# Attention of a hybrid decoder: fixed tiles for split transposes and probabilities, weights loaded one unit ahead, residual rows on VectorE

## The chip, the cores and the metric

The kernel runs on one core of a Trainium2 chip. The core has five engines that run their own instruction queues in order: TensorE (PE in the profile) for matrix products, VectorE (DVE), ScalarE (ACT), GpSimd (POOL) and SyncE (SP, which here only starts transfers). Data is worked on in the on-chip memory; matrix products land in eight accumulation banks. The metric is the device time of one execution in microseconds (us), lower is better.

## The reference

A trunk of two layers runs over 1024 tokens of width 1024 in float32. The even layer mixes with a pooling and a state-space part, the odd layer with two kinds of causal attention; behind each mixer stand a layer norm and a SwiGLU block (FFN) with another norm. The change touches the odd layer above all:

```python
def block_causal_attention(q, k, v, log_decay_cum):   # 8 heads of 64, twice
    ...
        sc = jnp.einsum('bhqd,bhkd->bhqk', qi, k).astype(F32) * scale
        if fi is not None:
            sc = sc + fi[..., :, None] - log_decay_cum[:, :, None, :]
        sc = jnp.where(kpos[None, :] <= qpos[:, None], sc, -jnp.inf)
        p = jax.nn.softmax(sc, axis=-1).astype(v.dtype)
        return jnp.einsum('bhqk,bhkd->bhqd', p, v)
...
    x = layer_norm(DEEPNORM_ALPHA * x + h, ln_mix_g[l], ln_mix_b[l])
    x = layer_norm(DEEPNORM_ALPHA * x + swiglu(x, ffn_w_gate[l], ffn_w_up[l], ffn_w_down[l]),
                   ln_ffn_g[l], ln_ffn_b[l])
```

The first kind of attention has a forget gate (the bias `log_decay_cum`), the second has its queries and keys unpacked from a low-rank latent.

## The kernel before

**Products.** Every float32 operand is split into a high and a low part by `split` or `operand`: ScalarE writes the high part (line 196), VectorE or GpSimd subtracts it from the source (line 204). Each product is then three matmuls: high by high, high by low, low by high (lines 237 to 239 in the projections, 499 to 501 and 635 to 637 in the FFN).

**The pool of slots.** One pool, `big`, of 50 slots of 128 x 1024 float32 holds nearly everything: raw weights `wr`, their parts `wh` and `wl`, probabilities `prob`, split transposes `pt`, squares `sq` for the norm of the latents, residual rows `resr`. A call of `slot` takes a new slot; the first instruction that writes it waits until all users of the slot's former tile are done. Each engine takes its queue in order, so such a wait holds up everything behind it on that engine.

**Attention.** `weave` interleaves two generators. `chain` goes through four pairs of heads of the first kind and four of the second; a step is a head and a block of 256 queries. `softmax` makes the scores (TensorE, line 1600), their minimum or maximum on VectorE, the exponential on ScalarE and the division on VectorE (line 1631). `pv` then transposes the probabilities on TensorE (line 1652), splits the transposes into a `pt` tile (or into the one fixed tile `diag` where the causal edge lies), and multiplies by the values (line 1670). `filler` supplies projection units for the heads to come; `preload` loads raw weights `ahead + dma_ahead` units ahead and splits them `ahead` units ahead. In time: the first kind of attention fills some 1230 to 1590 us of the trace, the second some 1590 to 1840.

**Residual rows.** The even layer's FFN left its normed rows without gain and offset in the DRAM tensor `store`. `late` loads each of the eight row blocks, multiplies by the gain, adds the offset (lines 442 and 443) and stores it again (line 444); `chain` calls it once in every second step from the second pair on. The odd layer's end reads the rows back as `acc` (line 1510).

**FFN.** `ffn` multiplies 2 x 2 blocks with seven products in place of eight. The product `step` takes its accumulation bank from `bank()`, which goes round a list; `second` is the down projection and begins with banks `p0` to `p3`.

Of the kernel before, what the change touches and what calls it, by code (L numbers as in the profile page):

```python
# [12 lines left out]
F32 = mybir.dt.float32  # L13
F32R = mybir.dt.float32r
BF16 = mybir.dt.bfloat16
AF = mybir.ActivationFunctionType
ALU = mybir.AluOpType
# [64 lines left out]
class Trunk:  # L82
# [67 lines left out]
    def turn(self, tags):  # L150
        self.turns[tags] = n = self.turns.get(tags, -1) + 1
        return self.ps(tags[n % len(tags)], 1)
# [238 lines left out]
    def finish(self, accs, gb, evac, ln=None, store=None, nxt=None, rows=None):  # L391
# [3 lines left out]
        nc = self.nc  # L395
# [41 lines left out]
        def late():  # L437
            v = self.ln_vecs(*gb)
            yield
            for t in range(NT):  # L440
                r = self.load_raw(store[t * P:(t + 1) * P, :], name="res")
                nc.gpsimd.tensor_tensor(out=r, in0=r, in1=v[0], op=ALU.mult)
                nc.gpsimd.tensor_tensor(out=r, in0=r, in1=v[1], op=ALU.add)
                nc.gpsimd.dma_start(out=store[t * P:(t + 1) * P, :], in_=r)
                yield
# [3 lines left out]
    def ffn(self, l, ln, store, rows, parts, nxt=None):  # L449
# [53 lines left out]
        hid = {}  # L503
        turn = itertools.cycle(("p0", "p1", "p2", "p3", "pa", "pa"))

# [717 lines left out]
    def odd(self, accs, store, spill, nxt, rows):  # L1223
# [350 lines left out]
        def filler():  # L1574
            self.grain = self.odd_grain
            misc_weight()
            self.preload(units, self.pre_n, ws)
            for g, u in zip(lead, units):
                yield from g
                done.add(u[0])  # L1580
            yield from spread(self.units_y(units, done, ws, 2), self.spread)
# [26 lines left out]
        def softmax(S, nF):  # L1608
            prob = []
            n = [x.shape[1] for x in S]  # L1610
            if sum(n) <= 1024:
                t = self.slot(name="prob")
                prs = [t[:, :n[0]], t[:, n[0]:n[0] + n[1]]]
            else:
                prs = [self.slot(name="prob")[:, :x] for x in n]
            l = self.small((P, 2), "l", bufs=6)
# [19 lines left out]
        for t in diag:  # L1636
            for c in (0, 512):
                nc.vector.tensor_copy(out=t[:, c:c + P], in_=self.zerob)

        def pv(prob, vv, u, ot, e):  # L1640
            nj = 2 * u + 2
            hl = {}

            def tr(jj):
                ps = self.pb()
                last = jj == u
                for y in range(2):
                    j = 2 * jj + y
                    for x in range(2):
                        c = (1 - y if last else y) * 256 + x * P  # L1650
                        if j <= 2 * u + x:
                            nc.tensor.transpose(out=ps[:, c:c + P], in_=prob[x][:, j * P:(j + 1) * P],  # L1652
                                                identity=self.ident)
                t = diag[self.turn_of("diag", self.n_diag)] if last else self.slot(dt=F32R, name="pt")
                b = P if last else 0
# [71 lines left out]
        def chain():  # L1727
# [4 lines left out]
            n = 0  # L1732
            for pr in pairs():
# [5 lines left out]
                for i, (e, u) in enumerate(self.steps[kind]):  # L1739
# [5 lines left out]
                    if pend and self.tr_first[kind]:  # L1745
                        next(pend[0])
                    if n and i % 2:
                        next(late, None)
# [143 lines left out]
```

## Time and profile before

| what | value |
|---|---|
| three executions, us | 2543.9, 2545.56, 2548.15 (median 2545.56) |
| the profiled execution, us | 2546.77 |
| its span in the trace, us | 2544.7 |
| TensorE busy, us (share of the span) | 2449.8 (96%) |
| VectorE | 1824.6 (72%) |
| ScalarE | 1044.6 (41%) |
| GpSimd | 758.2 (30%) |
| mean granted clock of TensorE | 0.986 of 2.4 GHz |

The span is the traced part of the profiled execution. The shares are means over the whole program; the stages differ. A granted clock of 1.00 stands for 2.4 GHz, and one near 0.50 for the lower level, 1.2 GHz. In the rows below, p and pa are accumulation banks, and `p<-pt,fv` names the tile that is written and those that are read.

### The profile page before, as it was taken

The numbers are of one execution on the slowest core, as the hardware profiler recorded it, in microseconds if no ns is written. First come the engines' busy times: TensorE is split into PE (matmuls) and PEld (weight loads), VectorE is DVE, ScalarE is ACT, GpSimd is POOL, SyncE is SP. The second block draws the span as 40 slices with busy tenths as digits, with TensorE's granted clock in tenths as the row PEclk, the third lists the DMA queues.
The fourth block names the chain that finished last, engine by engine and source line by source line (L and its number), as shares of the span: only waits on it lengthen the run. The fifth ranks groups of instructions, "written<-read, shape, count | busy, mean of one in ns | idle before, by whom it ended". The sixth has DMA issues, their size and how long they took to land. (4 is left out here: it accounts for less than half of the span.)

```text
span 2544.7 us, 31623 instructions
## 1 busy us (share of the span) xinstructions
PE 2449.8 (96%) x11886; PEld 2002.8 (79%) x11886; DVE 1824.6 (72%) x2907; ACT 1044.6 (41%) x1758; POOL 758.2 (30%) x446
## 2 busy tenths in 40 slices
PE   8999999999999999999998899998999999999998
PEld 6788877778888878887786777777877888887887
DVE  4365554788777779974645467787779778777988
ACT  3343344352222234454544356665544232233453
POOL 2454442113443441111113333111011433433113
PEclk9999999999999999999999899998999999999999
DMA  4111114124333347332011122012322433426641
GB/s 172 50 34 42 34 42 164 56 79 153 133 133 128 133 168 283 119 105 96 26 50 62 63 69 63 19 42 93 115 83 95 149 121 124 149 99 257 215 153 71
DMA packets 95257, 269.87 MB, mean 106 GB/s; under 512 B 9952, under 2 KB 10208, under 8 KB 95104
## 3 DMA queue, kind: packets, MB, share of 16 engines
q1 hardware_dynamic: 85632, 234.75, 26.8%
q0 software_dynamic: 6720, 23.13, 2.5%
q10 hardware_dynamic: 2752, 9.96, 1.1%
q8 instruction: 94, 1.54, 0.3%
q14 instruction: 59, 0.48, 0.1%
HBM read 190.08 MB, written 75.50 MB: 104 GB/s over the span
## 5 line engine op out<-in xcount | busy, mean ns | idle before, releaser
L204 DVE TENSOR_TENSOR w<-wr,w 128x512 fp32r<-128x512 f32 x440 | 415.7, 968 | 105.4 <-ACT w L196 99.6
L196 ACT CAST w<-wr 128x512 fp32r<-128x512 f32 x440 | 251.6, 619 | 424.2 <-DVE wr L482 331.7
L499 PE MATMUL p<-x,w 128*128 128x512 f32 x848 | 331.9, 393 | 6.4 <-ACT w L196 4.8
L500 PE MATMUL p<-x,w 128*128 128x512 f32 x848 | 331.2, 391 | 0.1
L501 PE MATMUL p<-x,w 128*128 128x512 f32 x848 | 331.2, 391 | 0.0
L547 POOL TENSOR_TENSOR h<-h,c 128x1024 f32<-128x1024 f32 x44 | 114.5, 2602 | 572.3 <-DVE c L540 420.2
L204 POOL TENSOR_TENSOR wl<-wr,wh 128x1024 fp32r<-128x1024 f32 (+2 forms) x55 | 128.2, 2333 | 358.7 <-ACT wh L196 292.0
L499 PEld LDWEIGHTS p<-x,w 128*128 128x128 f32 x848 | 159.7, 188 | 43.2 <-ACT w L196 6.3
L500 PEld LDWEIGHTS p<-x,w 128*128 128x128 f32 x848 | 159.8, 188 | 33.6 <-DVE x L204 1.2
L501 PEld LDWEIGHTS p<-x,w 128*128 128x128 f32 x848 | 159.7, 188 | 33.7 <-DVE w L204 0.8
L499 PE MATMUL pa<-x,w 128*128 128x512 f32 x384 | 149.4, 389 | 0.0
L500 PE MATMUL pa<-x,w 128*128 128x512 f32 x384 | 149.4, 389 | 0.0
L501 PE MATMUL pa<-x,w 128*128 128x512 f32 x384 | 149.4, 389 | 0.0
L239 PE MATMUL pa<-xh,wl 128*128 128x512 f32 x368 | 144.4, 392 | 4.4 <-POOL wl L204 4.4
L237 PE MATMUL pa<-xh,wh 128*128 128x512 f32 x368 | 146.7, 399 | 1.9 <-ACT u L904 1.1
L238 PE MATMUL pa<-xl,wh 128*128 128x512 f32 x368 | 144.1, 392 | 0.0
L635 PE MATMUL p<-w,h 128*128 128x512 f32 x352 | 136.9, 390 | 3.6 <-DVE c L542 3.6
L636 PE MATMUL p<-w,h 128*128 128x512 f32 x352 | 137.4, 391 | 1.9 <-DVE w L204 1.8
L637 PE MATMUL p<-w,h 128*128 128x512 f32 x352 | 136.8, 389 | 0.0
L204 DVE TENSOR_TENSOR h<-hr,h 128x512 fp32r<-128x512 f32 x154 | 123.4, 801 | 10.8 <-ACT h L196 10.7
L196 ACT CAST h<-hr 128x512 fp32r<-128x512 f32 x154 | 95.3, 619 | 73.9 <-DMA hr<-parts 37.6
L1652 PE MATMUL p<-con,prob 128*128 128x128 f32 x576 | 95.4, 283 | 8.6 <-DVE pt L204 4.9
(408 smaller groups left out, 6024.8 us busy)
## 6 DMA issues: line engine op xcount, KB each, us to landing
hr<-parts SPq DMA_DIRECT2D x70, 512.0 KB, 4.2
wr<-in_ffn_w_gate_dram SPq DMA_DIRECT2D x44, 512.0 KB, 3.8
wr<-in_ffn_w_up_dram SPq DMA_DIRECT2D x44, 512.0 KB, 4.2
wr<-in_ffn_w_down_dram SPq DMA_DIRECT2D x44, 512.0 KB, 8.8
parts<-s SPq DMA_DIRECT2D x80, 256.0 KB, 2.1
accr<-rows SPq DMA_DIRECT2D x32, 512.0 KB, 3.6
parts<-h SPq DMA_DIRECT2D x60, 256.0 KB, 2.1
wr<-in_even_wt_dram SPq DMA_DIRECT2D x24, 512.0 KB, 3.8
```

The lines of the kernel that those rows point to most:

```text
L196: self.nc.scalar.copy(out=out, in_=in_)
L204: eng.tensor_tensor(out=out, in0=in_, in1=hi.bitcast(F32), op=ALU.subtract)
L237: mm(out=out, lhsT=lh, rhs=rh, start=i == 0, stop=False)
L238: mm(out=out, lhsT=lh, rhs=rl, start=False, stop=False)
L239: mm(out=out, lhsT=ll, rhs=rh, start=False, stop=i == n - 1)
L499: mm(out=out, lhsT=ah, rhs=b[k][:, lo], start=k == 0, stop=False)
L500: mm(out=out, lhsT=ah, rhs=b[k][:, hi], start=False, stop=False)
L501: mm(out=out, lhsT=al, rhs=b[k][:, lo], start=False, stop=k == 3)
L547: pt(out=h, in0=h, in1=c, op=ALU.mult)
L635: mm(out=out, lhsT=ah, rhs=b[:, lo], start=first, stop=False)
L636: mm(out=out, lhsT=ah, rhs=b[:, hi], start=False, stop=False)
L637: mm(out=out, lhsT=al, rhs=b[:, lo], start=False, stop=last)
```

## The change

Five edits: `late` computes on VectorE instead of GpSimd, with a yield between its two instructions, and is called at every step; the list of banks in `ffn` begins two places later; `dma_ahead` is 1 instead of 2 from the odd layer on; two `pt` tiles and four `prob` tiles are allocated once and taken in turn.

```diff
@@ late
             for t in range(NT):
                 r = self.load_raw(store[t * P:(t + 1) * P, :], name="res")
-                nc.gpsimd.tensor_tensor(out=r, in0=r, in1=v[0], op=ALU.mult)
-                nc.gpsimd.tensor_tensor(out=r, in0=r, in1=v[1], op=ALU.add)
+                nc.vector.tensor_tensor(out=r, in0=r, in1=v[0], op=ALU.mult)
+                yield
+                nc.vector.tensor_tensor(out=r, in0=r, in1=v[1], op=ALU.add)
                 nc.gpsimd.dma_start(out=store[t * P:(t + 1) * P, :], in_=r)
                 yield
@@ ffn
-        turn = itertools.cycle(("p0", "p1", "p2", "p3", "pa", "pa"))
+        turn = itertools.cycle(("pa", "pa", "p0", "p1", "p2", "p3"))
@@ odd, filler
             self.grain = self.odd_grain
+            self.dma_ahead = 1
             misc_weight()
@@ odd, softmax
-                t = self.slot(name="prob")
+                t = turn("prob")
                 prs = [t[:, :n[0]], t[:, n[0]:n[0] + n[1]]]
             else:
-                prs = [self.slot(name="prob")[:, :x] for x in n]
+                prs = [turn("prob")[:, :x] for x in n]
@@ odd
+        kept = {n: [self.slot(dt=d, name=n) for _ in range(c)] for n, d, c in (("pt", F32R, 2), ("prob", F32, 4))}
+
+        def turn(n):
+            if not kept[n]:
+                return self.slot(dt=F32R if n == "pt" else F32, name=n)
+            return kept[n][self.turn_of(n, len(kept[n]))]
@@ odd, pv
-                t = diag[self.turn_of("diag", self.n_diag)] if last else self.slot(dt=F32R, name="pt")
+                t = diag[self.turn_of("diag", self.n_diag)] if last else turn("pt")
@@ odd, chain
-                    if n and i % 2:
+                    if n:
                         next(late, None)
```

**ScalarE in the second pair of heads.** A row names line, operation, the tile written and those read; the number behind a name tells one tile from another, and the brackets hold the engines and transfer queues whose progress the instruction waits for (Pool is GpSimd, DMASW a transfer that GpSimd started, DMAHW one of another queue). Before:

```order
L196 CAST wh_10360<-wr_9762 128x1024 [waits DMAHW7_49,PE_49]
L1395 ACTIVATE sq_10170<-p_1586_10285 128x512 [waits DVE_49]
L196 CAST pt_10378<-p_1604_10373 128x512 [waits Pool_49]
L196 CAST diag_8972<-p_1606_10394 128x384 [waits PE_49]
L1674 COPY otmp_10420<-p_1593_10323 64x256 [waits PE_49]
L1623 ACTIVATE prob_10440,l_10442<-prob_10440,nm_10443 128x640 [waits DVE_49]
L1623 ACTIVATE prob_10441,l_10442<-prob_10441,nm_10446 128x768 [waits DVE_49,Activation_49]
L196 CAST pt_10455<-p_1617_10450 128x512 [waits DMASW1_49,PE_49,Pool_49]
L196 CAST diag_8972<-p_1620_10473 128x384 [waits PE_49,Activation_49]
```

After, at the same place in the program:

```order
L196 CAST pt_8976<-p_1573_10318 128x512 [waits PE_49]
L1396 ACTIVATE sq_10150<-p_1565_10265 128x512 [waits DVE_49]
L196 CAST pt_8975<-p_1580_10352 128x512 [waits PE_49,Activation_49]
L196 CAST diag_8972<-p_1581_10372 128x384 [waits PE_49]
L1683 COPY otmp_10398<-p_1571_10304 64x256 [waits PE_49]
L1625 ACTIVATE prob_8977,l_10416<-prob_8977,nm_10417 128x640 [waits DVE_49]
L196 CAST pt_8976<-p_1590_10424 128x512 [waits PE_49,Activation_49]
L1625 ACTIVATE prob_8978,l_10416<-prob_8978,nm_10420 128x768 [waits DVE_49]
L196 CAST diag_8972<-p_1592_10446 128x384 [waits PE_49,Activation_49]
```

The `pt` rows wait for TensorE and ScalarE alone, where they waited for GpSimd and for a transfer that GpSimd had started; `wh` and the square have moved against them by a few places.

**GpSimd and VectorE at a residual row.** Before, GpSimd had both instructions of a row block (the first `resr` here), ahead of the square and of the weight's low part:

```order
L204 TENSOR_TENSOR wl_10361<-wr_9762,wh_10360 128x1024 [waits DMAHW2_49,DMAHW1_49,DMAHW3_49,DVE_49,DMAHW7_49,PE_49,Activation_49]
L442 TENSOR_TENSOR resr_10423<-resr_10423,lnv_10245 128x1024 [waits DMAHW3_49,DMASW7_49,PE_49]
L443 TENSOR_TENSOR resr_10423<-resr_10423,lnv_10247 128x1024 [waits DMASW0_49,Pool_49]
L444 DMA store<-resr_10423 128x1024 [waits Pool_49]
L1402 TENSOR_TENSOR sq_10170<-sq_10170,sq_10365 128x1024 [waits Activation_49]
L204 TENSOR_TENSOR wl_10541<-wr_10163,wh_10540 128x1024 [waits DMAHW0_49,PE_49,Activation_49]
```

After, VectorE has them (here the second block), and GpSimd keeps the store alone:

```order
L1623 ISA prob_8977,nm_10585<-pa_10577,nF_10172 128x384 [waits PE_49]
L1623 ISA nm_10585 128x1
L204 TENSOR_TENSOR pt_8976<-p_1607_10525,pt_8976 128x512 [waits Activation_49]
L442 TENSOR_TENSOR resr_10401<-resr_10401,lnv_10180 128x1024 [waits DMAHW7_49,DMAHW3_49,Pool_49]
L204 TENSOR_TENSOR diag_8972<-p_1608_10548,diag_8972 128x384 [waits Activation_49]
L444 TENSOR_TENSOR resr_10401<-resr_10401,lnv_10182 128x1024 [waits DVE_49]
L1684 TENSOR_TENSOR ot_10179<-p_1599_10499,otmp_10571 64x256 [waits Activation_49]
L1623 ISA prob_8977,nm_10588<-pa_10577,nF_10172 128x512
L1623 ISA nm_10588 128x1
```

The multiplication stands on VectorE directly behind the low part of a `pt` tile and ahead of that of the `diag` tile, and waits for its load (DMAHW); the addition follows one row later.

**ScalarE at the first weights of the output projection (around 1726 us before).** Units whose raw operand is loaded from `spill` by ScalarE's own queue alternate with units loaded by SyncE. Before:

```order
L196 CAST wh_13886<-wr_13330 128x1024 [waits DMAHW6_49]
L225 DMA wr_13890<-spill 128x1024
L196 CAST wh_13892<-wr_13698 128x1024 [waits DMAHW7_49]
L1674 COPY otmp_13945<-p_2302_13853 64x256 [waits PE_49]
L196 CAST wh_13898<-wr_13884 128x1024 [waits DMAHW1_49]
L225 DMA wr_13902<-spill 128x1024
L196 CAST wh_13904<-wr_13890 128x1024 [waits DMAHW2_49]
L196 CAST wh_13910<-wr_13896 128x1024 [waits DMAHW3_49]
L196 CAST wh_13914<-wr_13902 128x1024 [waits DMAHW4_49]
L196 CAST wh_13918<-wr_13908 128x1024 [waits DMAHW5_49]
L1626 ACTIVATE prob_13960,l_13961<-pa_13951,nm_13962 128x128 [waits DVE_49,Activation_49]
L196 CAST pt_13974<-p_2336_13969 128x512 [waits Pool_49]
```

After:

```order
L225 DMA wr_13735<-spill 128x1024
L196 CAST wh_13737<-wr_13557 128x1024 [waits DMAHW6_49,Pool_49]
L1683 COPY otmp_13798<-p_2156_13706 64x256 [waits PE_49]
L1628 ACTIVATE prob_8979,l_13813<-pa_13804,nm_13814 128x128 [waits DVE_49]
L196 CAST pt_8976<-p_2188_13821 128x512 [waits PE_49]
L196 CAST wh_13743<-wr_13735 128x1024 [waits DMAHW0_49]
L196 CAST pt_8975<-p_2189_13834 128x512 [waits PE_49]
L225 DMA wr_13747<-spill 128x1024
L196 CAST wh_13749<-wr_13741 128x1024 [waits DMAHW1_49]
L1628 ACTIVATE prob_8979,l_13813<-pa_13804,nm_13817 128x256 [waits DVE_49]
L196 CAST pt_8976<-p_2191_13853 128x512 [waits DVE_49,PE_49]
L196 CAST wh_13755<-wr_13747 128x1024 [waits DMAHW2_49]
```

The seven `wh` rows stood nearly in one piece, with both loads from `spill` ahead; with one unit less ahead, each load is issued later and its `wh` follows a few rows behind it, and exponentials and `pt` rows of the attention stand in between.

## Rows read from the trace of the kernel before

**Rows 1.** The page of the profile, its first part.

```profile
PE 2449.8 (96%) x11886; PEld 2002.8 (79%) x11886; DVE 1824.6 (72%) x2907; ACT 1044.6 (41%) x1758; POOL 758.2 (30%) x446
```

**Rows 2.** Busy time by engine in stretches of the attention; PEclk is the granted clock.

```profile
1230.00:1420.00 190.00, 176.19 (x998) 142.65 (x997) 110.11 (x218) 90.46 (x181) 46.74 (x25) 0.97 0.17 56
...
1420.00:1590.00 170.00, 152.31 (x786) 120.35 (x784) 109.11 (x198) 87.26 (x164) 58.53 (x42) 0.95 0.20 59
...
1590.00:1700.00 110.00, 103.56 (x622) 85.81 (x623) 83.21 (x155) 69.95 (x153) 18.40 (x9) 0.98 0.08 26
```

**Rows 3.** The chain of waits, TensorE, 1230 to 1600 us: total us, times, longest.

```profile
PE p L1670 <- ACT pt L196: 12.3, 8, 3.1
...
PE p L1652 <- DVE pt L204: 4.9, 4, 2.5
```

**Rows 4.** The same, ScalarE (ACT), 1230 to 1600 us.

```profile
ACT pt L196 <- POOL wl L204: 9.9, 4, 3.5
...
ACT pt L196 <- DMA store<-resr: 6.0, 1, 6.0
```

**Rows 5.** Timeline of TensorE: first matmul behind a gap, gap and releaser in brackets.

```profile
1329.29 0.39 PE L1670 MATMUL p<-pt,fv 128*128 128x256 f32 x1 [1.33 <-ACT pt L196]
...
1343.29 0.39 PE L1670 MATMUL p<-pt,fv 128*128 128x256 f32 x1 [3.06 <-ACT pt L196]
...
1352.80 0.39 PE L1670 MATMUL p<-pt,fv 128*128 128x256 f32 x1 [1.43 <-ACT pt L196]
...
1365.88 0.58 PE L1670 MATMUL p<-pt,fv 128*128 128x256 f32 x1 [3.01 <-ACT pt L196]
...
1590.52 0.39 PE L1670 MATMUL p<-pt,fv 128*128 128x256 f32 x1 [2.48 <-ACT pt L196]
```

**Rows 6.** Timelines of ScalarE and TensorE around 1440 us.

```profile
1440.12 1.04 ACT L196 CAST wh<-wr 128x1024 fp32r<-128x1024 f32 x1 [5.17 <-DMA store<-resr]
...
1442.08 0.58 PE L1670 MATMUL p<-diag,fv 128*128 128x256 f32 x1 [3.72 <-ACT diag L196]
...
1445.98 0.37 PE L1411 MATMUL p<-ones,sq 128*128 128x2 f32 x1 [1.48 <-POOL sq L1402]
```

**Rows 7.** Timelines of GpSimd, VectorE and TensorE around 1472 us.

```profile
1471.51 2.40 POOL L442 TENSOR_TENSOR resr<-resr,lnv 128x1024 f32<-128x1024 f32 x1 [25.59 <-DMA resr<-store]
...
1472.35 1.78 DVE L1631 TENSOR_SCALAR prob<-prob,l 128x384 f32<-128x384 f32 x1
...
1478.51 0.47 PE L1652 MATMUL p<-con,prob 128*128 128x128 f32 x1 [2.45 <-DVE pt L204]
```

**Rows 8.** Busy time and granted clock in three short stretches.

```profile
1300.00:1320.00 20.00, 20.00 (x109) 15.19 (x108) 8.78 (x22) 10.05 (x22) 3.42 (x3) 1.00 0.21 79
...
1367.00:1373.00 6.00, 5.46 (x19) 3.82 (x17) 4.07 (x8) 4.32 (x10) 2.05 (x1) 0.55 0.34 87
...
1440.00:1454.00 14.00, 10.44 (x37) 9.07 (x38) 4.55 (x14) 6.21 (x11) 4.67 (x2) 0.53 0.00 1
```

**Rows 9.** The tile of the residual rows: ns min/median/max of its instructions, and its loads.

```profile
L442 POOL TENSOR_TENSOR resr<-resr,lnv x8: 2356/2404/2839, 1334.3 to 1526.1; 128x1024 f32<-128x1024 f32 x8
...
DMA to landing us min/median/max: 2.9/3.5/5.1
```

**Rows 10.** VectorE, two tiles: ns min/median/max of their instructions.

```profile
L1631 DVE TENSOR_SCALAR prob<-prob,l x128: 277/554/2799, 1229.6 to 1821.9; 128x128 f32<-128x128 f32 x16, 128x256 f32<-128x256 f32 x16, 128x896 f32<-128x896 f32 x16, 128x1024 f32<-128x1024 f32 x16
...
L204 DVE TENSOR_TENSOR wl<-wr,wh x16: 1215/1222/3380, 9.1 to 1827.0; 128x1024 fp32r<-128x1024 f32 x16
```

**Rows 11.** Timelines of TensorE at the start of the second FFN phase, layer 0.

```profile
943.12 0.50 PE L635 MATMUL p<-w,h 128*128 128x512 f32 x1 [1.82 <-DVE c L542]
...
951.61 0.50 PE L636 MATMUL p<-w,h 128*128 128x512 f32 x1 [0.90 <-DVE w L204]
```

**Rows 12.** Timelines of ScalarE and TensorE around 1734 us.

```profile
1734.43 1.05 ACT L196 CAST wh<-wr 128x1024 fp32r<-128x1024 f32 x1 [3.59 <-DMA wr<-spill]
...
1734.14 0.72 PE L238 MATMUL p<-wl,wh 128*128 128x512 f32 x1 [2.11 <-DVE wl L204]
```


## Prediction

> **What bounds it now.** I read the shares first: TensorE is busy for 96% of the span [rows 1], so no other engine is the bound, and a gain can only come from TensorE's gaps and from stretches at a low clock. Then I read the stages in which the change acts. From 1230 to 1590 us TensorE works 176.19 of 190 and 152.31 of 170 us, so it is idle for 31.5, at a granted clock of 0.97 and 0.95; from 1590 to 1700 it is 0.98 [rows 2]. VectorE is busy there for 219.2 of 360 us (61%), GpSimd for 105.3 (29%). Then I read what TensorE waits for: the longest wait is for the high part of a split transpose (`pt`, ScalarE), 12.3 us, then its low part (VectorE), 4.9 [rows 3]. The reader is to see next that ScalarE isn't slow there: it is held up itself. Its `pt` writes waited 9.9 us for GpSimd to finish a weight's low part and 6.0 us for a store of residual rows [rows 4]. Neither has a part in the attention; they are former owners of the slot that the new `pt` got. Five gaps of TensorE follow from such waits: 1.33, 3.06, 1.43, 3.01 and 2.48 us [rows 5], 11.3 us in all. A sixth place is like them: `wh` waits 5.17 us for a store of residual rows, and TensorE stands for 3.72 and 1.48 us behind it [rows 6].
>
> The clock is the other half. At 1300 to 1320 us the granted clock is 1.00 and TensorE has no gap; right behind the gap of 3.01 us the clock from 1367 to 1373 is 0.55, and behind the 3.72 us it is 0.53 for 14 us [rows 8], which is the level of 1.2 GHz.
>
> **The change, part by part.**
>
> *Fixed `pt` and `prob` tiles.* A fixed tile has only attention's instructions as former users. The order shows those waits of `pt` rows as gone; what is left is TensorE's reading two tiles earlier, which stands ahead of the transposes that the same row waits for anyway. So the 11.3 us of [rows 5] go. Four `prob` tiles hold two steps of two tiles, and no more than two steps are in flight, so I price new waits there at nothing; the cover is TensorE's order, in which a step's transposes end before the step after the next begins.
>
> *Residual rows off GpSimd.* GpSimd loses 16 instructions of 2.40 us [rows 9], 38.4 us, and the stores come earlier, so a slot that residual rows had is free sooner. I take the 5.2 us of [rows 6] as removed. A second gain is a collision: while GpSimd multiplies a residual row from 1471.51, VectorE's division of `prob` takes 1.78 us, and `pt` and TensorE follow 2.45 us late [rows 7]. That goes too: 2.5 us.
>
> The price is on VectorE. The nearest row, a subtraction of the same size with both inputs in on-chip memory, takes 1.22 us as a rule and 3.38 at most [rows 10]; 16 of them are 19.5 us. VectorE is idle for 39% of the stretch, so some hide, but a row stands in the order between the low part of `pt` and that of `diag`, and delays whatever is behind it. The lower bound is 0; the upper takes all on the path and lets GpSimd meet one in five (it is busy for 105.3 − 38.4 = 66.9 of 360 us afterwards), 16 × (1.22 + 0.19 × 2.16) = 26 us. I take 4, near the lower end, because all waits of TensorE for `pt`'s low part together are only 4.9 us [rows 3] with 219 us of work on VectorE: a part of about 2% of it, and at the places with rows more.
>
> What the trace shows of the collision is that a `prob` division takes 0.55 us at the median and 2.80 at most, a subtraction 1.22 and 3.38 [rows 10]. The Trainium skill ("SBUF — State Buffer", section "Who interferes with whom") says that a VectorE instruction with two inputs in SBUF contends with a GpSimd instruction that reads SBUF, and that the one that comes second blocks fully until the first is done; the maxima agree. By that rule the edit exchanges one collision for another, since the new instructions have two such inputs: if each met a GpSimd instruction, they would cost 16 × (1.22 + 2.40) = 58 us, and with all of that on the path the sum at the end would be +39 instead of −15.
>
> Each multiplication waits for its own load, which lands 2.9 to 5.1 us after issue [rows 9], and now everything behind it on VectorE waits too. Before, GpSimd waited there. The same call of `late` issues a load and its multiplication, but SyncE starts the load as soon as its slot is free, and VectorE has the rows of the step before to do until then. For eight waits the bounds are 0 and 8 × 3.5 = 28; I take 3, one wait's length, because SyncE has little else to issue in this stretch and some ten rows of VectorE stand ahead of a multiplication.
>
> *What takes the slots' place.* `wh`, squares and latents still draw from the pool, which has six slots fewer to go round; about six such rows in the order have a GpSimd instruction or store as a former owner not far ahead. The nearest price is 5.17 us on ScalarE with 5.2 on TensorE [rows 6]. Bounds: 0, and three such places, 15.6. I take 6, one place and a little, and 3 more for the clock behind them.
>
> *One unit ahead.* It frees a slot and issues loads later. The place where it can decide is the start of the output projection: before, `wh` waits 3.59 us for a load from `spill` and TensorE stands for 2.11 us there [rows 12]. After, three such loads stand on ScalarE, each a few rows ahead of its `wh` (two are in the piece of the order); but attention's rows stand in between. Gains and losses are both possible: −7 (the gaps around the block go) to +8 (three gaps like 2.11 and some clock). I take 0.
>
> *Banks.* The second FFN phase begins with `p0` to `p3`; the last products now lie in `pa`, so the wait of 1.82 us goes. But 8 us later a wait of 0.90 for a weight's low part stands on VectorE [rows 11], whose queue is full up to there; TensorE comes there 1.82 us earlier and waits 2.7 instead. Bounds for both layers −3.6 and +3.4 (a clock fall behind each longer gap); I take +1.
>
> *The clock.* Stretch times (1 − clock) is 190 × 0.03 + 170 × 0.05 + 110 × 0.02 = 16.4 us [rows 2]. Idle time at a low clock costs nothing, and TensorE was busy for 10.44 of 14 and 5.46 of 6 us in the two stretches of [rows 8], so I take 0.8 of it, 13 us. The lower bound is 0, if other gaps of over 2 us take the old ones' place.
>
> *The sum.* −11.3 − 5.2 − 2.5 − 13 = −32.0; +4 + 3 + 6 + 3 + 0 + 1 = +17; in all −15 us. The profiled execution would go from 2546.77 to 2531.8, and the median of the runs shown, 1.2 us below it, from 2545.56 to 2530.5. A measurement of this kernel can tell about 0.2%, 5 us, from no change.
>
> **The rivals.**
>
> *Nearly all of it stays.* VectorE's rows hide, and the slots left over don't bind: −32 + 4 = −28, 2517. For it: TensorE's waits for VectorE are short. Against: the pool has been short of slots at six places already, and there are fewer of them.
>
> *The waits move.* ScalarE's queue is held by `wh`, squares and latents instead of `pt`, since a `wh` that waits delays the `pt` behind it as before ([rows 6] is that case). Three places at 5.2 and the clock kept low (13 not gained): −32 + 13 + 15.6 + 3 = about 0, 2545. For it: the owners that were waited for remain; against: GpSimd's queue is shorter by 38.4 us and gives slots back earlier.
>
> *Slower: VectorE's queue is stopped by residual rows.* The multiplication waits for its load in front of a `pt` or `diag` row that TensorE needs. It decides if the eight blocks cost TensorE over 32/8 = 4 us each: a load's 3.5 us and a blocked pair of 1.22 + 2.40 and 1.22 do. With 8 × 5 = 40 us and the 32 gained this gives +8, 2554. For it: load and use are issued by one call, and the maxima of [rows 10]. Against: 39% idle time on VectorE and projection matmuls that TensorE can do meanwhile. The blocking is the rule of the Trainium skill ("SBUF — State Buffer", "Who interferes with whom") weighed above.
>
> **How the numbers follow.** The forecast (2524 to 2539 by its own bounds) gets 0.52, nearly all 0.14, no change 0.17, slower 0.17. Faster by over 0.2% holds the first two and a part of the third: 0.70; within 0.2%: 0.14; slower: 0.16. The range leaves out the tails of the outer cases: 2513, a little below the second case, to 2553, short of the slower case's middle.
>
> **What would show it.** In the changed trace: no `pt` write of ScalarE waits for GpSimd or a store; TensorE is idle for about 15 us from 1230 to 1590 instead of 31.5; the clock there is 0.98 or higher; residual rows on VectorE take 1.2 us, with some up to 3.4, and wait under 1 us on average for their loads; the second FFN phase has one gap of about 2.7 us instead of two. It would be wrong if VectorE shows idle time in front of `resr` of over 2 us at most blocks, if ScalarE's waits reappear at `wh`, or if the output projection's start shows gaps of over 7 us in all.

## The result and the profile after

The changed kernel takes 2511.28 us (median of four runs, 2506.76 to 2515.03) against 2545.53: a ratio of 0.9864, interval 0.9844 to 0.9884, 34 us faster. The prediction had 2530.5 and a range down to 2513: the sign was right, the size was less than half, and the measured time lies below the range. The first part of the page of the profiled execution:

```profile
span 2511.4 us, 31611 instructions
...
PE 2437.8 (97%) x11886; PEld 2000.8 (80%) x11886; DVE 1825.7 (73%) x2923; ACT 1046.5 (42%) x1758; POOL 716.9 (29%) x430
```

The whole gain lies in the odd layer. The first fence has the window of that layer in the kernel before, up to the start of the next FFN, the second the same piece of work after (its first columns: start, end, length, then busy time of TensorE with its matmuls in brackets; the third number from the end is the granted clock):

```profile
1180.00:1911.00 731.00, 675.25 (x3730) 549.06 (x3728) 491.81 (x939) 374.88 (x731) 157.10 (x92) 0.96 0.19 61
```

```profile
1180.00:1877.00 697.00, 662.13 (x3729) 542.29 (x3728) 494.15 (x956) 377.58 (x733) 117.27 (x77) 0.98 0.20 65
```

731 us have become 697. TensorE's idle time went from 731 − 675.25 = 55.8 to 697 − 662.13 = 34.9 us, which is 20.9 of the 34; the same 3730 matmuls (3729 recorded) took 13.1 us less, because the granted clock rose from 0.96 to 0.98. All that is outside of this window took 2544.7 − 731 = 1813.7 us before and 2511.4 − 697 = 1814.4 after.

The stretches that answer to [rows 2], by the same windows' columns:

```profile
1230.00:1400.00 170.00, 164.61 (x948) 135.49 (x947) 105.96 (x215) 84.22 (x171) 27.23 (x16) 0.97 0.17 56
...
1400.00:1570.00 170.00, 161.42 (x868) 128.32 (x867) 121.04 (x230) 98.41 (x185) 39.77 (x33) 0.98 0.22 66
...
1570.00:1680.00 110.00, 104.24 (x630) 86.87 (x629) 86.05 (x156) 71.19 (x152) 19.67 (x10) 0.98 0.09 28
```

From 1230 to 1570 TensorE is idle for 14.0 us, where [rows 2] had 31.5 from 1230 to 1590; the pieces match only roughly (1816 matmuls here, 1784 there). GpSimd is busy for 67.0 us instead of 105.3, VectorE for 227.0 (67%) instead of 219.2, in 20 us less. What answers to [rows 3] and [rows 4], TensorE's and ScalarE's waits from 1230 to 1600 us (total, times, longest):

```profile
PE p L1679 <- DVE diag L204: 3.9, 4, 2.8
...
PE p L1661 <- DVE pt L204: 2.1, 3, 1.5
...
PE p L1679 <- ACT pt L196: 1.5, 3, 0.7
```

```profile
ACT rb L1423 <- POOL wl L204: 3.7, 1, 3.7
...
ACT wh L196 <- POOL sq L1403: 2.1, 1, 2.1
```

The wait for a `pt` tile's high part is 1.5 us, from 12.3. No `pt` write of ScalarE waits for GpSimd or for a store any more; these two rows show that other tiles still do, for 3.7 and 2.1 us (`rb` and `sq` belong to the norm of the latents), though TensorE waits for `rb` for only 0.7 us. The residual rows, which answer to [rows 9], now as VectorE's instructions (ns min/median/max), with VectorE's wait for their loads:

```profile
L442 DVE TENSOR_TENSOR resr<-resr,lnv x8: 1217/1226/3404, 1316.5 to 1476.8; 128x1024 f32<-128x1024 f32 x8
...
L444 DVE TENSOR_TENSOR resr<-resr,lnv x8: 1209/1224/2819, 1317.8 to 1481.5; 128x1024 f32<-128x1024 f32 x8
...
  DMA resr<-store: 5.3, 2
...
DMA to landing us min/median/max: 2.9/3.6/4.6
```

They take 1.22 us as a rule and at most 3.40, as the subtraction of [rows 10]; VectorE waited for two of the eight loads, 5.3 us in all. Last, the place of [rows 11] in the changed kernel: the timeline, and the window behind it.

```profile
953.16 0.80 PE L637 MATMUL p<-w,h 128*128 128x512 f32 x1 [3.01 <-DVE w L204]
```

```profile
952.80:956.30 3.50, 3.14 (x8) 2.52 (x9) 3.43 (x5) 0.00 (x0) 3.48 (x6) 0.52 0.47 150
```

The two gaps of 1.82 and 0.90 us are one of 3.01, and 3.5 us at a clock of 0.52 follow.

### The profile page after: what moved, and what is told of

It reads as the page before. It is cut to its first block, busy times and chain, and to the rows that moved or that the text cites. A ratio compares the mean times of both kernels' runs of the same rounds, so it can differ in the third digit from the quotient of the medians.

```text
span 2511.4 us, 31611 instructions
## 1 busy us (share of the span) xinstructions
PE 2437.8 (97%) x11886; PEld 2000.8 (80%) x11886; DVE 1825.7 (73%) x2923; ACT 1046.5 (42%) x1758; POOL 716.9 (29%) x430
## 3 DMA queue, kind: packets, MB, share of 16 engines
q8 instruction: 94, 1.54, 0.3%
## 5 line engine op out<-in xcount | busy, mean ns | idle before, releaser
L500 PE MATMUL p<-x,w 128*128 128x512 f32 x832 | 325.8, 393 | 6.9 <-ACT w L196 6.9
L501 PE MATMUL p<-x,w 128*128 128x512 f32 x832 | 325.0, 391 | 0.0
L502 PE MATMUL p<-x,w 128*128 128x512 f32 x832 | 324.9, 391 | 0.0
L500 PEld LDWEIGHTS p<-x,w 128*128 128x128 f32 x832 | 157.1, 189 | 39.8 <-ACT w L196 7.9
L502 PEld LDWEIGHTS p<-x,w 128*128 128x128 f32 x832 | 156.9, 189 | 33.2 <-DVE w L204 0.6
L501 PEld LDWEIGHTS p<-x,w 128*128 128x128 f32 x832 | 157.1, 189 | 32.4
L500 PE MATMUL pa<-x,w 128*128 128x512 f32 x400 | 155.8, 389 | 0.0
L501 PE MATMUL pa<-x,w 128*128 128x512 f32 x400 | 155.6, 389 | 0.0
L502 PE MATMUL pa<-x,w 128*128 128x512 f32 x400 | 155.6, 389 | 0.0
L636 PE MATMUL pa<-w,h 128*128 128x512 f32 x264 | 102.8, 389 | 0.0
```

Source lines behind the costliest of these rows:

```text
L500: mm(out=out, lhsT=ah, rhs=b[k][:, lo], start=k == 0, stop=False)
L501: mm(out=out, lhsT=ah, rhs=b[k][:, hi], start=False, stop=False)
L502: mm(out=out, lhsT=al, rhs=b[k][:, lo], start=False, stop=k == 3)
L636: mm(out=out, lhsT=ah, rhs=b[:, lo], start=first, stop=False)
```

## The experiments

Each ratio is to the kernel before on the same chip, with its 95% interval; times in us are compared by these ratios, since the runs are from several chips. The edits to the changed kernel come first in the table, then those to the kernel before.

| run | what it is | ratio | interval | us to before (2546) |
|---|---|---|---|---|
| the change | as shown | 0.9864 | 0.9844 to 0.9884 | −35 |
| after_again | the same, in a later comparison | 0.9863 | 0.9846 to 0.9881 | −35 |
| a_no_kept | no fixed tiles | 0.9889 | 0.9876 to 0.9901 | −28 |
| a_no_pt | only `prob` fixed | 0.9894 | 0.9881 to 0.9906 | −27 |
| a_no_prob | only `pt` fixed | 0.9926 | 0.9914 to 0.9939 | −19 |
| a_no_res | residual rows as before | 0.9914 | 0.9902 to 0.9926 | −22 |
| a_gps_pace | the same with the new calls | 0.9911 | 0.9893 to 0.9929 | −23 |
| a_no_math | residual rows without arithmetic | 0.9839 | 0.9820 to 0.9859 | −41 |
| a_no_res_math | the same with the old calls | 0.9830 | 0.9811 to 0.9850 | −43 |
| a_no_bank | old list of banks | 0.9853 | 0.9841 to 0.9866 | −37 |
| old_banks_again | the same, in a later comparison | 0.9861 | 0.9847 to 0.9875 | −35 |
| a_ahead0 | old banks, nothing loaded further ahead | 0.9887 | 0.9873 to 0.9901 | −29 |
| dve_late | old banks, residual rows in the second attention | 0.9890 | 0.9876 to 0.9904 | −28 |
| pool_late | the same on GpSimd | 0.9942 | 0.9928 to 0.9955 | −15 |
| b_ahead | before, one unit ahead alone | 0.9953 | 0.9941 to 0.9965 | −12 |
| b_res | before, residual rows alone | 0.9924 | 0.9906 to 0.9941 | −19 |
| ba_49 | b_ahead with 49 slots | 1.0023 | 1.0015 to 1.0032 | +6 |

**One edit undone or alone.** Theory A was the prediction's: the fixed tiles carry the gain. The rivals: GpSimd's relief carries it (B), or one unit ahead (C).

Without fixed tiles (a_no_kept):

```diff
-        kept = {n: [self.slot(dt=d, name=n) for _ in range(c)] for n, d, c in (("pt", F32R, 2), ("prob", F32, 4))}
+        kept = {n: [self.slot(dt=d, name=n) for _ in range(c)] for n, d, c in (("pt", F32R, 0), ("prob", F32, 0))}
```

> The changed kernel with probabilities and transposes in slots of the pool again; the rest of the change stays. Theory A (the fixed tiles carry the gain, because they alone take ScalarE's transposes out of the waits for slots): most of the 34 us come back, 2531 to 2540 us. Theory B (GpSimd's relief carries it: with 38 us less to do it finishes the weights' low parts early, so that slots are free in time whoever takes them): 2511 to 2517 us. Theory C (one unit ahead carries it, since it gives slots back): also 2511 to 2517.

Measured: 2519.46, ratio 0.9889, only 0.0025 or 6 us more than with them, with intervals that overlap. Theory A falls: four fifths of the gain don't need the fixed tiles.

The traces show where the fixed tiles' share lies. From the first transposition of the attention to the first product of the output projection a_no_kept takes 473.3 us and the changed kernel 471.3; from there to the FFN the difference is three times as large. The first row is the kernel before, the second a_no_kept, the third the changed kernel; behind them TensorE's wait for weights in the same windows, without the fixed tiles and with them:

```profile
1728.69:1890.27 161.58, 150.49 (x782) 122.08 (x781) 123.53 (x232) 77.05 (x147) 20.00 (x12) 0.95 0.27 90
```

```profile
1701.61:1860.32 158.71, 147.36 (x771) 118.67 (x772) 123.00 (x232) 77.45 (x147) 18.55 (x12) 0.96 0.27 94
```

```profile
1704.29:1856.67 152.38, 145.02 (x772) 117.97 (x771) 119.46 (x232) 76.48 (x146) 17.95 (x12) 0.99 0.28 98
```

```profile
PE p L238 <- DVE wl L204: 6.7, 4, 2.1
```

```profile
PE p L238 <- DVE wl L204: 1.8, 2, 1.5
```

158.7 us become 152.4. (Ahead of the attention, where the two kernels are the same, the trace of the changed kernel is 4.7 us longer; that of after_again is not, and has 151.4 us here.) In a_no_kept, as in b_ahead, ScalarE's `wh` rows still stand nearly in one piece there, each second one behind its load from `spill`; TensorE has four gaps of 1.1 to 2.1 us, and the clock is at its lower level for 13.7 us. So the rows of the attention that stand between the `wh` rows after the change come with the fixed tiles, not with one unit less ahead. Why fixed tiles change that order was not followed.

Residual rows as before (a_no_res):

```diff
-                nc.vector.tensor_tensor(out=r, in0=r, in1=v[0], op=ALU.mult)
-                yield
-                nc.vector.tensor_tensor(out=r, in0=r, in1=v[1], op=ALU.add)
+                nc.gpsimd.tensor_tensor(out=r, in0=r, in1=v[0], op=ALU.mult)
+                nc.gpsimd.tensor_tensor(out=r, in0=r, in1=v[1], op=ALU.add)
...
-                    if n:
+                    if n and i % 2:
```

> The changed kernel with the residual rows on GpSimd again, in every second step; the rest stays. Theory A: 3 to 8 us slower than the changed kernel (the collision of 2.5 us, the store that held a weight's slot, 5.2, less what VectorE gets back), 2514 to 2519. Theory B: 2530 or more. Theory C: 2511 to 2516.

Measured: 2524.83, 0.9914: 13 us given back, more than A and less than B said.

Old list of banks (a_no_bank):

```diff
-        turn = itertools.cycle(("pa", "pa", "p0", "p1", "p2", "p3"))
+        turn = itertools.cycle(("p0", "p1", "p2", "p3", "pa", "pa"))
```

> The changed kernel with the old list of banks. All theories: the gap of 3.01 us at the start of both second FFN phases is two gaps of 1.8 and 0.9 again, and the low clock of 3.4 us behind it goes, 1.7 us each: 2 to 4 us faster, 2507 to 2509. If the bank edit was a gain in itself: 2513 to 2515.

Measured: 2509.56, 0.9853. The intervals overlap with the change's, so it was run again further down.

One unit ahead alone (b_ahead), on the kernel before:

```diff
             self.grain = self.odd_grain
+            self.dma_ahead = 1
```

> The kernel before with one unit ahead alone. Theory A and B: within 4 us of before, 2542 to 2549. Theory C: most of the gain, 2520 or less. In between, if it has only the 6 us that the changed kernel gains at the start of the output projection: 2538 to 2541.

Measured: 2534.18, 0.9953: 12 us by one number, the edit that the prediction had at 0, and outside all three forecasts. None of A, B and C holds alone. ScalarE's waits for GpSimd in this run, 1230 to 1600 us, and TensorE's for `pt`:

```profile
ACT pt L196 <- POOL wl L204: 4.3, 2, 2.6
...
ACT wh L196 <- POOL sq L1402: 2.6, 1, 2.6
...
ACT pt L196 <- POOL ql L204: 2.4, 1, 2.4
```

```profile
PE p L1671 <- ACT pt L196: 5.6, 3, 2.3
```

The store of residual rows is no longer waited for by `pt` or `wh`, the weights' low parts for 4.3 instead of the 9.9 us of [rows 4], and TensorE's wait is 5.6 instead of 12.3. No fixed tile is in this kernel. That the waits went because other tiles stand in the slots is what the next run tests.

**Is it the slots?** ba_49 takes a slot away from that kernel:

```diff
-        self.big = ctx.enter_context(tc.tile_pool(name="big", bufs=50))
+        self.big = ctx.enter_context(tc.tile_pool(name="big", bufs=49))
...
             self.grain = self.odd_grain
+            self.dma_ahead = 1
```

> The kernel before with one unit ahead, and 49 slots in the pool instead of 50. Theory S (one unit ahead gains its 12 us because a raw weight less stands in the pool, so that each new tile meets an owner that is one tile older): the slot that is taken away takes most of it back, 2541 to 2549. Theory L (it gains because loads and low parts are issued later and collide less): as with 50 slots, 0.995 of before, 2532 to 2538.

Measured: 2551.99, 1.0023. The slot takes all of it back and 6 us more. The time alone would also fit a lost slot that costs 18 us whatever the loads do, since the kernel before was not run with 49 slots; the trace decides for theory S, since it shows the same waits, gap by gap. Here are ScalarE's waits, then the first matmuls behind three of TensorE's gaps.

```profile
ACT pt L196 <- POOL wl L204: 9.9, 4, 3.5
...
ACT pt L196 <- DMA store<-resr: 5.9, 1, 5.9
...
ACT wh L196 <- DMA store<-resr: 5.3, 1, 5.3
```

```profile
1345.70 0.38 PE L1671 MATMUL p<-pt,fv 128*128 128x256 f32 x1 [2.92 <-ACT pt L196]
...
1369.33 0.39 PE L1671 MATMUL p<-pt,fv 128*128 128x256 f32 x1 [3.01 <-ACT pt L196]
...
1445.08 0.58 PE L1671 MATMUL p<-diag,fv 128*128 128x256 f32 x1 [3.89 <-ACT diag L196]
```

The reader is to compare this with [rows 4] and [rows 5]: 9.9 us in four waits, the longest 3.5, as before; 5.9 and 5.3 for 6.0 and 5.17; gaps of 2.92, 3.01 and 3.89 for 3.06, 3.01 and 3.72, in the same places a few us later. A raw weight less ahead and a slot less cancel: by these rows each new tile meets the same former owner as in the kernel before. One load fewer ahead gains because each tile's owner is one tile older, not because of the loads. The windows from the first transposition of the attention to the first product of the output projection say the same (the kernel before, b_ahead, ba_49):

```profile
1230.38:1728.69 498.31, 458.24 (x2559) 370.94 (x2558) 325.93 (x612) 266.24 (x532) 127.28 (x76) 0.97 0.17 53
```

```profile
1229.58:1716.33 486.75, 453.13 (x2567) 368.88 (x2566) 322.73 (x612) 266.56 (x532) 126.70 (x76) 0.98 0.17 54
```

```profile
1232.17:1732.92 500.75, 457.49 (x2567) 369.84 (x2566) 327.31 (x612) 266.22 (x532) 126.87 (x76) 0.97 0.17 53
```

498.3 us become 486.8, most of the gain of b_ahead, and are 500.8 again with 49 slots. The 6 us beyond are spread over the program and not explained; the slot is missing in all of it, while one unit less is loaded ahead in the odd layer alone.

**Residual rows alone, and what in them counts.** b_res is the change's edit of `late` and of its call, on the kernel before:

```diff
-                nc.gpsimd.tensor_tensor(out=r, in0=r, in1=v[0], op=ALU.mult)
-                nc.gpsimd.tensor_tensor(out=r, in0=r, in1=v[1], op=ALU.add)
+                nc.vector.tensor_tensor(out=r, in0=r, in1=v[0], op=ALU.mult)
+                yield
+                nc.vector.tensor_tensor(out=r, in0=r, in1=v[1], op=ALU.add)
...
-                    if n and i % 2:
+                    if n:
```

> The kernel before with the residual rows on VectorE at the new pace, nothing else. Theory D (each of the three edits removes waits for slots by itself, and they overlap; the residual edit earns 13 to 19 us because GpSimd's queue gets short): 2527 to 2535. Theory E (the residual edit works only with the pool relieved by one unit less ahead): within 4 us of before, 2542 to 2549.

Measured: 2528.3, 0.9924, 19 us without any other edit. With the 12 of b_ahead that makes 31, and a_no_kept, which has both (and the new list of banks), is at 28: these two nearly add up. Theory E falls. ScalarE's longest wait for GpSimd in this run and TensorE's for `pt`, 1230 to 1600 us:

```profile
ACT pt L196 <- POOL wl L204: 10.1, 4, 3.6
```

```profile
PE p L1671 <- ACT pt L196: 9.2, 8, 3.1
```

The 9.9 us of [rows 4] for a weight's low part are still there. What went are ScalarE's two waits for a store of residual rows and, with them, TensorE's gaps of 3.06 and 1.43 us in [rows 5] and 3.72 in [rows 6], and the 2.45 of the collision in [rows 7]: 10.7 us (the 1.48 of [rows 6] is still 1.41). The 13.7 us at the lower clock from 1440.7 us on are 3.4.

a_gps_pace leaves the new calls and puts the arithmetic on GpSimd:

```diff
-                nc.vector.tensor_tensor(out=r, in0=r, in1=v[0], op=ALU.mult)
+                nc.gpsimd.tensor_tensor(out=r, in0=r, in1=v[0], op=ALU.mult)
                 yield
-                nc.vector.tensor_tensor(out=r, in0=r, in1=v[1], op=ALU.add)
+                nc.gpsimd.tensor_tensor(out=r, in0=r, in1=v[1], op=ALU.add)
```

> The changed kernel with the two instructions of a residual row on GpSimd, but called as in the changed kernel (a yield between them, every step). Theory D: it is GpSimd's time that counts, 2522 to 2528, like the run with the old calls. Theory F (the earlier start of the rows and their even spread do it): 2511 to 2516.

Measured: 2524.26, 0.9911: it is the engine, not the calls; theory F falls. The two programs differ in nothing but the engine of the two instructions, so this pair shows what GpSimd's time does. Timelines of GpSimd, ScalarE and TensorE around 1390 us, and the window behind:

```profile
1386.76 2.46 POOL L442 TENSOR_TENSOR resr<-resr,lnv 128x1024 f32<-128x1024 f32 x1 [16.18 <-DMA resr<-store]
...
1389.29 2.37 POOL L444 TENSOR_TENSOR resr<-resr,lnv 128x1024 f32<-128x1024 f32 x1
...
1391.62 2.33 POOL L204 TENSOR_TENSOR wl<-wr,wh 128x1024 fp32r<-128x1024 f32 x1
```

```profile
1393.99 0.59 ACT L1701 COPY nF<-p 128x512 f32<-128x512 f32 x1 [3.92 <-POOL wl L204]
```

```profile
1394.63 0.79 PE L1699 MATMUL p<-mix,sel 40*128 40x512 f32 x1 [3.38 <-ACT nF L1701]
```

```profile
1393.00:1407.00 14.00, 12.37 (x29) 7.88 (x30) 3.62 (x11) 4.71 (x10) 1.50 (x2) 0.51 0.09 37
```

Two residual instructions stand ahead of a weight's low part on GpSimd; the low part starts at 1391.62 and ends at 1393.95. The bias row `nF` has drawn the slot that this instruction was a user of: ScalarE waits 3.92 us for it, TensorE 3.38, and the clock is 0.51 for the next 14 us. In the changed kernel the same `nF` group waits 0.4 us for GpSimd. So the fixed tiles don't end such waits; they pass to whichever tile draws the slot next, and here GpSimd's shorter queue ends them. A second way is in the traces: VectorE's instructions other than the residual rows, between the first transposition and the output projection's first product, take 318.2 us in a_gps_pace and 305.5 in the changed kernel (325.9 before, 312.2 in b_res), which fits fewer collisions with GpSimd's instructions. How the 12 us divide between slots and collisions was not separated.

Without the arithmetic, with new calls (a_no_math) and old ones (a_no_res_math, its edit shown against a_no_res):

```diff
-                nc.vector.tensor_tensor(out=r, in0=r, in1=v[0], op=ALU.mult)
                 yield
-                nc.vector.tensor_tensor(out=r, in0=r, in1=v[1], op=ALU.add)
```

> The changed kernel with the residual rows' multiplication and addition left out: a row block is loaded and stored as it is, so the residual lacks the gain and the offset. Its distance to the changed kernel is the price on VectorE: the prediction had 4 us and 3 for the loads, so 2504 by it; by theory D next to nothing, 2508 to 2512; all on the path would be 2490.

```diff
-                nc.gpsimd.tensor_tensor(out=r, in0=r, in1=v[0], op=ALU.mult)
-                nc.gpsimd.tensor_tensor(out=r, in0=r, in1=v[1], op=ALU.add)
```

> The same arithmetic left out with the old calls of the residual rows: neither GpSimd nor VectorE has it, the rest of the change stays. Theory D: as fast as the changed kernel or up to 5 us faster, 2506 to 2512, since GpSimd's 38 us are what the old rows cost. Theory F: slower by what the late start costs, 2518 to 2526.

Measured: 2507.22 (0.9839) and 2504.43 (0.9830). Both are a little faster than theory D said, and a_no_math lies between its range and the 2504 that follow from the prediction; theory F falls once more. On VectorE the arithmetic costs 0.0025 or 6 us, its waits for loads included, with intervals that overlap; on GpSimd, against a_no_res, 0.0084 or 21 us for 38.4 us of work on an engine that is busy for 29% of the span.

**Which fixed tiles.** a_no_pt and a_no_prob set one of the two counts to 0:

> The changed kernel with the split transposes in slots of the pool again, the probabilities in their four fixed tiles. By the prediction's reading (ScalarE's waits at the transposes): all that the fixed tiles bring is lost, 0.989 of before, and more, since the pool has four slots less to go round: 2519 to 2526. If the probabilities are what counts: 0.9865, 2511 to 2515.

> The changed kernel with the probabilities in slots of the pool again, the transposes in their two fixed tiles. By the prediction's reading: 0.985 to 0.987 of before, 2508 to 2514, the probabilities' tiles bring nothing. If they count: 0.989, 2517 to 2520.

Measured: 2519.89 (0.9894), as with no fixed tiles at all; and 2529.23 (0.9926), 9 us worse than with none. The first is as the prediction's reading had it; the second is outside both forecasts and against that reading: the transposes' tiles alone harm. VectorE's waits in a_no_prob, 1230 to 1600 us, GpSimd's instruction that it waits for, and TensorE's longest gap:

```profile
DVE prob L1623 <- POOL wl L204: 4.1, 2, 3.6
...
DVE prob L1623 <- POOL sq L1403: 2.8, 1, 2.8
```

```profile
1435.99 2.33 POOL L204 TENSOR_TENSOR wl<-wr,wh 128x1024 fp32r<-128x1024 f32 x1 [5.71 <-DMA store<-resr]
```

```profile
1440.68 0.37 PE L1412 MATMUL p<-ones,sq 128*128 128x2 f32 x1 [5.58 <-POOL sq L1403]
```

The low part of a weight has drawn the slot of a residual row and waits 5.71 us for its store, and GpSimd with it. The `prob` tile of a step has drawn a slot that this low part still uses, and the square that TensorE waits 5.58 us for stands behind it on GpSimd. Pinning some tiles shifts the others; what it gains depends on who meets whom then. This reading is of one trace; why the slots fell to these tiles was not followed through the whole program.

**Further versions.** Nothing loaded beyond what is split (a_ahead0), with the old banks:

```diff
-            self.dma_ahead = 1
+            self.dma_ahead = 0
```

> The changed kernel with the old list of banks and no unit loaded ahead beyond the one that is split ahead. Theory S: another slot is free, but a load of 4 us now stands between its issue and the split of the same unit, on ScalarE; with 0.985 for the old list of banks and one ahead, 0.982 to 0.986 if slots still bind, 0.990 or more if the loads come too late. I expect the latter, 2520 to 2530.

Measured: 2517.69, 0.9887, between the two forecasts, and 7 to 9 us worse than the same with one unit ahead. ScalarE's waits for loads, 1180 to 1800 us:

```profile
ACT wh L196 <- DMA wr<-in_odd_wt_dram: 3.7, 3, 1.6
...
ACT wh L196 <- DMA wr<-in_w_u_dram: 1.2, 1, 1.2
```

The changed kernel has no wait of ScalarE for these two loads. That they make up the loss is argued, not shown.

Residual rows in the second kind of attention, on GpSimd (pool_late) and on VectorE (dve_late), both with the old banks:

```diff
-                    if n:
+                    if n >= 4:
                         next(late, None)
```

> The changed kernel with the old banks and the residual rows on GpSimd, but called in the second kind of attention, where GpSimd is busy for 20 of 110 us. If GpSimd's time costs only through slots and low parts in the first kind: near the kernel without the arithmetic less the banks' 2 us, 2500 to 2508. If GpSimd's time costs wherever it is: 2515 to 2525.

> The same with the residual rows on VectorE in the second kind of attention, where VectorE is busy for 78% of the time (86 of 110 us): slower than with them in the first kind (69%) if their price is VectorE's queue, 2511 to 2518; the same as with the old banks alone, 2508 to 2511, if it has room there too.

(pool_late has GpSimd's two instructions of a_no_res as well.) Measured: 2531.94 (0.9942) and 2519.36 (0.9890), against 0.9861 with the rows in the first kind. Both are slower than either of their forecasts; I had expected gains on GpSimd, which has little to do there. GpSimd, ScalarE and TensorE around 1656 us of pool_late:

```profile
1648.63 2.39 POOL L442 TENSOR_TENSOR resr<-resr,lnv 128x1024 f32<-128x1024 f32 x1 [4.92 <-DMA resr<-store]
...
1651.10 2.51 POOL L443 TENSOR_TENSOR resr<-resr,lnv 128x1024 f32<-128x1024 f32 x1
```

```profile
1656.26 0.83 ACT L196 CAST wh<-wr 128x768 fp32r<-128x768 f32 x1 [6.42 <-POOL resr L442]
```

```profile
1658.14 0.58 PE L1601 MATMUL pa<-kh,qh 128*128 128x256 f32 x1 [6.17 <-ACT prob L1627]
```

ScalarE's wait for a weight's high part ends with the last of the eight multiplications (it follows these two on GpSimd, from 1653.57 to 1656.22). A row block would be held longer, for the addition and the store; the tile that is free at this point is the gain's, which all eight rows read, so the high part has most likely drawn its slot. TensorE stands for 6.17 us behind it. A low busy share of GpSimd doesn't make it a cheap place; by this gap, what counts is which slots its work holds, and for how long. That this gap and its like make up the loss is argued, not shown.

The banks again, beside the changed kernel:

> The changed kernel with the old list of banks once more, beside the next one: 2 to 4 us faster than it, by the lower clock behind one gap of 3 us in each layer.

> The changed kernel as it is, beside the one with the old banks: 0.986 to 0.987 of the kernel before, 2509 to 2514 us.

Measured: 0.9861 and 0.9863. The bank edit makes no difference that these runs can tell, so no version was found that beats the changed kernel clearly.

Not tried: fixed tiles with two units ahead, so what one unit ahead is worth beside the fixed tiles is not known; fixed tiles alone on the kernel before; and more than 50 slots.

## Why the prediction was half right

The forecast was 15 us less, and 34 were measured. Three terms of its sum failed: "One unit ahead" at 0 (12 us alone), "Residual rows off GpSimd" at 7.7 (19 alone, 13 beside the rest), and "What takes the slots' place" at a loss of 9 (TensorE's idle time leaves no room for it). What the prediction read as the limit was right.

**Right.** What bounds the stage (TensorE's gaps from waits for slots and from a collision, and the clock behind them) is what the change took most of away: the gaps of the odd layer fell by 20.9 us. Most of the signs that the prediction named came: no `pt` write waits for GpSimd or a store, TensorE is idle for 14.0 us where it said about 15, the loads cost VectorE 5.3 us or 0.7 for each, and the two gaps of the FFN became one of 3.01. VectorE's price was put at 4 us and 3 for the loads; the run without the arithmetic says 6 for both together. The maximum of 3.40 us belongs to a row (1476.76) that starts 0.04 us behind a GpSimd square of 2.37 us, and 2.37 + 1.22 is 3.59. This agrees with the Trainium skill ("SBUF — State Buffer", "Who interferes with whom"), by which the second of two such instructions is blocked until the first is done. The banks' cost is too small to be measured.

**Luck: the clock.** It gave 13.1 us in the odd layer, and the prediction had 13, but in other places. Its 13 were 0.8 of the 16.4 us that the stretches of [rows 2] lose; the three stretches that answer to them still lose 170 × 0.03 + 170 × 0.02 + 110 × 0.02 = 10.7. The larger part came behind them, from the first product of the output projection on: 161.58 × 0.05 = 8.1 us before, 152.38 × 0.01 = 1.5 after, a stretch that the clock term left out.

**Wrong: "One unit ahead ... I take 0."** The prediction looked at one place, the loads from `spill`. The edit's effect is on the whole pool: 12 us alone, through the slots (b_ahead, ba_49), and nearly all of it ahead of that place, where b_ahead gains under 1 us (161.6 to 160.9).

**Wrong: "Residual rows off GpSimd".** It was priced by the two places where residual rows showed up themselves, 5.2 and 2.5 us. But the gap of 3.06 us behind a store of residual rows [rows 4] and the 1.43 behind it were booked to the fixed tiles, and b_res removes them without any: 10.7 us of gaps in all where 7.7 were priced, and a part of the low clock besides. The 9.9 us of ScalarE's waits for a weight's low part, which it leaves, don't explain its gain. The edit is worth 13 us with the fixed tiles and 19 without.

**Wrong: "What takes the slots' place", +6 and +3.** ScalarE's waits for GpSimd and stores at `wh`, `nF`, latents and the like are 16.2 us when the residual rows stay on GpSimd (a_gps_pace, where TensorE stands for 3.38 us at `nF`) and 10.2 in the changed kernel, where they cost TensorE little. The rival in which the waits move was a real mechanism; the second edit of the same change takes most of its effect away. The sum also did not fit its own sign: with these 6 us and the 4 and 3 for VectorE, 31.5 − 19 would leave TensorE idle for 25.5 us, not for the 15 that the prediction named; 14.0 were measured.

**Not as told: the fixed tiles.** They got 11.3 us and a part of the clock in the sum, all in the attention. Taken away last they are worth 6 (0.9864 and 0.9889, with intervals that overlap), and in the traces 2 us of gain lie in the attention up to the output projection's first product and 6 behind it, at the place that the prediction priced at 0 under "One unit ahead". The two `pt` tiles, on which the reading of ScalarE's waits rested, are worth less than nothing by themselves. The edits compete for the same gaps: of the 12.3 us that TensorE waits for `pt` in [rows 3], b_res leaves 9.2 and b_ahead 5.6, both without a fixed tile. Taken one after the other the runs give 19 us (b_res), 9 more with one unit ahead and the banks (a_no_kept), and 6 more with the fixed tiles. The sum of −15 without the 9 us and with 12 in place of 0 would be −36, close to the 34 measured; with the other two terms wrong that is a coincidence. Of the rivals, the one in which nearly all of the gain stays (2517, chance 0.14) came nearest.

## What to carry to other kernels

Where one ring of buffers serves tiles of many kinds, a wait in the profile names the tile that happened to draw the slot; the cause is the owner that gives it back late. Two remedies worked here without pinning a tile: to shorten the queue of the owner's engine (19 us), and to have one tile less outstanding (12 us). Price such an edit over all tiles that draw from the ring, not at the place where the wait shows, and test it by taking one slot away. Edits that touch the ring don't add up by themselves: run each alone and each undone, and look in the traces at which stage each gain lies.

## What was not expected of the hardware

A gap of TensorE of 3.38 us is followed by 14 us at a granted clock of 0.51 in a_gps_pace, one of 3.01 us by 3.5 us at 0.52 in the changed kernel's FFN: what a gap costs by the clock varies, and the runs don't show why. The prediction's bound for the clock spoke of gaps of over 2 us; in the changed kernel the clock also fell behind one of 1.54, and stayed low for 10.2 us:

```profile
1347.71 0.66 PE L1661 MATMUL p<-con,prob 128*128 128x128 f32 x4 [1.54 <-DVE pt L204]
```

```profile
1348.70:1358.90 10.20, 8.68 (x31) 6.80 (x30) 8.21 (x14) 4.48 (x10) 0.56 (x1) 0.50 0.22 88
```

In the odd layer the clock gave 13.1 us of the 34.
